# Score products of the recurrence as two half-width products per chunk instead of one full-width product

## The chip, the cores and the metric

The kernel runs on one core of one Trainium2 chip. The metric is the device time of one execution in microseconds (us), as the median of several runs. Each engine of the core has an instruction queue of its own that runs in order; in the profile PE is TensorE (matrix products), PEld its weight loads, DVE VectorE, ACT ScalarE, POOL GpSimd, SP SyncE, which issues most DMAs.

## The reference

Two layers of a diffusion backbone, in float32. Each layer mixes 768 tokens (256 context, 512 latent) through three parallel head groups (a gated recurrence in both directions, differential attention, a Fourier mix), and then runs a SwiGLU block. Only the recurrence matters here. Cut to its core, for one head (K = V = 128) and one direction:

```
def hgrn2_scan(q, v, z, lb, s0, reverse):
    f = lb + (1.0 - lb) * jax.nn.sigmoid(z)
    k, log_f = 1.0 - f, log(f)
    ...
def step(state, inp):                       # one chunk of tokens
    bcum = jnp.cumsum(gi, axis=2)
    o_inter = (qi * exp(bcum)) @ state
    decay = exp(where(incl, bcum[t] - bcum[s], -inf))
    scores = einsum('bhtk,bhsk,bhtsk->bhts', qi, ki, decay)
    o_intra = scores @ vi
    state = state * exp(blast) + (ki * exp(blast - bcum)).T @ vi
```

`scores[t, s]` has a decay that depends on both tokens and on the feature k, so it is no single matrix product.

## The kernel before

Every tensor lives in one SBUF arena that is cut into nine regions; `reg2f`, `reg6f` and so on in the profile are these regions (the digit is the region, f or r the kind of its contents), and `P` is PSUM, eight banks of 512 float32 columns. Large projections split each float32 operand into a high and a low float32r part and make three products per contraction block (`mm3`): these are the rows with `reg7r` (the weight stream's split pieces) and 256 or 512 columns. Weights come from HBM as 512 KB pieces in a fixed sequence, through three raw slots that ACT and DVE split (`pump`).

**The recurrence.** The kernel takes chunks of 128 tokens and builds both directions together. `gla_levels(h)` forms the 128x128 score block of each chunk by seven doubling levels: at level `lev`, with s = 2^lev, the pairs (t, s') whose indices differ first at bit `lev` take their score from a product of decayed keys and decayed queries; a mask per level says which entries of the block they are, and `copy_predicated` (line 787) lays them into the score block `osc`. Ahead of level 0 one more product per chunk gives the diagonal (`dst(1, c)`, put into `osc` by a plain ACT copy). So a head has one initial set of products, levels 0 to 5, and level 6: eight sets. A set makes one product for each chunk: six chunks in layer 0, four in layer 1. There are four heads and two layers.

The products of the initial set and of levels 0 to 5 are 128x128x128 in plain float32: the stationary operand is 128 keys of a chunk (`KM`, interleaved from the two directions by an ACT copy, `mixed`), the moving operand 128 queries read from `QP` by the view `dims`, runs of s words taken in turn from two places that lie s + T words apart (T = 768). The initial set reads `q` contiguously. At level 6 only the two quarters of the block off the diagonal have entries, and the kernel already makes them as two 64x64 products per chunk, with contiguous operands, into two partition halves of the bank. At all lower levels the entries that the mask takes lie in the two 64x64 quarters on the diagonal.

Between sets, DVE multiplies keys and queries by the gates, ACT interleaves the next `KM`, DVE lays the scores in. A plain float32 product is recorded as two MATMUL records (two passes), so a set of six full products shows as x12, and one of twelve half products as x24.

**Order of the work.** The program is recorded by generators. `drive` runs a main line (projections) and advances side lanes (`gla_levels`, `gla_post`, preparation of attention, attention, modulation) when a planner, the class `Clock`, says that their operands will be there. `mm` tells the planner what a product costs. `now` is the planner's time of PE. These numbers set only where independent instructions stand in each queue. `gla_post` runs after the levels of a head: transposes of keys, the states of the chunks, and `scores @ v` (rows with `reg5f`). `gemv` computes the modulation vectors of the next stage on PE from weight pieces of its own in the same stream (rows `32x512`).

Of the kernel before, what the change touches and what calls it, by code (L numbers as in the profile page):

```python
# [19 lines left out]
T = SEQ + CTX  # L20
# [9 lines left out]
# arena (float32 words per partition)  # L30
# [14 lines left out]
class Layout:  # L45
    """Constant area at the end of the arena."""
# [31 lines left out]
class Clock:  # L78
    """Expected times of the engines (ns); they only decide the order in which independent work is issued."""

    # from the end of a result to its use, by the engine that uses it
# [7 lines left out]
    def cells(self, ap):  # L89
        """tensor name and words of an access pattern"""  # L90
        dims = [(d[0], d[1]) for d in ap.ap]
        key = (ap.tensor.name, ap.offset, tuple(dims))
        if key not in self.known:
            ps = dims[0][0]
            starts, width = [ap.offset % ps if ps else ap.offset], 1
            for st, n in dims[1:]:
                if st >= 64 and n <= 16:
                    starts = [o + st * i for o in starts for i in range(n)]
                else:
                    width += st * (n - 1)  # L100
            idx = np.unique(np.concatenate([np.arange(o, o + width) for o in starts]))
            self.known[key] = (ap.tensor.name, idx)
        return self.known[key]
# [37 lines left out]
    def free(self, b):  # L141
        """when the tensor engine can write a bank that the other engines used"""
        return max([v for e, v in self.bank.get(b, {}).items() if e != 'pe'], default=0.0) + self.LAT['pe']

    def written(self, ap):
        """when the tensor engine can read it"""
        name, idx = self.cells(ap)
        return float(self.of(self.w, name)[idx].max()) + self.LAT['pe']


class Builder:
    def __init__(self, tc, ctx, ins, out):
        self.tc, self.nc, self.ins, self.out = tc, tc.nc, ins, out
        nc = self.nc
        gp = ctx.enter_context(tc.tile_pool(name="arena", bufs=1))
        pp = ctx.enter_context(tc.tile_pool(name="psum", bufs=1, space=bass.MemoryType.PSUM))
        self.L = Layout()
        self.gp = gp
        # (start, end, kind): r regions feed float32r products and are written rounded only
        cuts = [A0, A0 + 6144, B0, B0 + 6144, C0, VB, X0, W0, RAW0, self.L.end]  # L160
        self.reg = [[a, b, None, None] for a, b in zip(cuts, cuts[1:])]
        for i, k in enumerate('rrfffffrf'):
            self.mode(i, k)
        self.M = gp.tile([128, 7, 128], U8, name="M")
        self.P = pp.tile([128, 4096], F32, name="P")
        p0 = self.P[:, 0:1]
        self.pt, self.poff, self.pps = p0.tensor, p0.offset, p0.ap[0][0]
        self.sides = []
        self.ck = Clock()
        self.ready = {}  # L170
        self.have, self.gated = set(), set()

# [1 line left out]
    def mode(self, i, k):  # L174
        """Region i starts over with another kind of contents."""
        a, b, _, old = self.reg[i]
        if old != k:
            t = self.gp.tile([128, b - a], F32, tag=f"reg{i}", name=f"reg{i}{k}")
            self.reg[i] = [a, b, t, k]
# [42 lines left out]
    def mm(self, out, lhsT, rhs, start=True, stop=True):  # L222
        n, m = self.cols(rhs), self.cols(lhsT)
        if rhs.dtype == F32R:
            t = max(0.417 * n, 105)
        elif m == 32:
            t = 0.5 * n
        elif m == 64 and n == 64:
            t = 112
        else:  # L230
            t = 425 if n < 96 else max(215, 1.69 * n)
        self.ck.op('pe', t, [out], [lhsT, rhs])
        self.nc.tensor.matmul(out, lhsT, rhs, start=start, stop=stop)  # L233
# [61 lines left out]
    def rsqrt_mean(self, dst, src, n, w):  # L295
        """dst = (src / n + eps) ** -0.5 on w columns."""
        g, mh = self.nc.gpsimd, self.S(self.L.mh, w)
        self.ck.op('po', 160, [dst], [src])
        g.tensor_scalar(out=dst, in0=src, scalar1=1.0 / n, scalar2=EPS, op0=ALU.mult, op1=ALU.add)
        self.pool(dst, dst, mh, ALU.pow, 300 + 165 * w)  # L300

# [1 line left out]
    def step(self, lane):  # L303
        """Advance one lane of side work; it is due again when its results are expected."""
        self.ck.last = 0.0
        try:
            r = next(lane[0])
            self.ready[id(lane)] = r or self.ck.last
        except StopIteration:
            lane.pop(0)  # L310
# [18 lines left out]
    def drive(self, main, drain=True):  # L329
        for c in main:  # L330
            if isinstance(c, float):
                # side work goes first while a bank is still being read
                while c > self.now:
                    b = self.due(True)
                    if b is None or b[0] >= c:
                        break
                    self.step_any()
                continue
# [8 lines left out]
            n = 0  # L347
# [74 lines left out]
    def pump(self, upto=-1):  # L422
        seq, go = self.seq, True
        while go:
# [9 lines left out]
            if (self.n_proc < self.n_dma and seq[self.n_proc][2] < self.n_freed + NW  # L434
# [6 lines left out]
                if self.sides[2] and self.nbk == 2:  # L441
                    # VectorE is the busier one beside the attention
                    self.pool(self.r(self.S(w + 1024, 1024)), rw, self.S(w, 1024), ALU.subtract, 1920)
                else:
                    self.tt(self.r(self.S(w + 1024, 1024)), rw, self.S(w, 1024), ALU.subtract)
# [4 lines left out]
    def get(self):  # L450
        """Next split piece of the stream: offset of its high part (low part 1024 further)."""
# [28 lines left out]
    def extra_time(self):  # L480
        """when its next step can run, if that is known"""
# [12 lines left out]
    def more(self, n=1, force=False):  # L494
        """Take steps of the modulation that runs beside the main line."""
# [14 lines left out]
    def gemv(self, mods, src, free, b, wr):  # L510
        """silu(cond) @ w_mod[l][:, m] as feature columns; one step per piece and per result."""
# [33 lines left out]
    def gemv_v(self, mods, src, free, b, acc):  # L545
        """the same beside the main line: products and partial sums on VectorE, sums over the partitions at the end"""
# [44 lines left out]
    def gate(self, l, m, goff, after=None):  # L591
        """gate * norm_g broadcast over the partitions."""
# [16 lines left out]
    def norm(self, t, junk):  # L609
        """reciprocal root mean squares of a token tile"""  # L610
# [7 lines left out]
    def normed(self, t):  # L618
        """when they are there"""
        return self.ck.written(self.S(self.L.st + t, 1)) - 250  # L620

    def scaled(self, t, y):
        """normalized tile"""
# [4 lines left out]
    def turned(self, y):  # L628
        """when the tensor engine can turn it"""
        return max(self.ck.written(self.S(o, 512)) for o in y)  # L630

    def turn(self, y, b0, b1):
        """feature-major"""
# [33 lines left out]
    def spare(self):  # L667
        """bank that the modulation leaves to short work"""
        return 3 if self.nbk == 2 and self.extra is None and not self.sides[2] else self.aux()

    def aux(self):
        """bank for short work beside an accumulation of the main line"""
# [49 lines left out]
    def osc(self, h, c):  # L722
        """score block of chunk c"""
# [5 lines left out]
    def gla_levels(self, h):  # L729
# [26 lines left out]
        yield  # L756
        for c in chunks:
            self.mm(dst(1, c), self.S(self.osc(h, c), 128), self.S(q + c * 128, 128))
# [5 lines left out]
        for lev in range(7):  # L764
            s = 1 << lev
            nb = T // (2 * s)
            dims = ((2 * s, 64 // s), (s + T, 2), (1, s))
            for c in chunks:
# [5 lines left out]
                else:  # L774
                    self.mm(dst(lev, c), self.S(KM + 128 * c, 128), self.V(QP + 128 * c, *dims))
# [97 lines left out]
    def prep(self, b):  # L873
        """rope and exact split of k0, q0, k1, q1"""
# [26 lines left out]
    def stack(self, b):  # L901
        """per head and map: high and low parts in three blocks of 32 rows"""
# [8 lines left out]
    def attention(self):  # L911
# [18 lines left out]
        def scores(i):  # L930
# [3 lines left out]
            # the second map starts within a bank while the modulation holds bank 3  # L934
# [107 lines left out]
    def mixer(self):  # L1042
# [17 lines left out]
        for h in range(4):  # L1060
            if l and h == 2:
                # work that needs no buffer of the recurrence
# [45 lines left out]
        for b in range(4):  # L1108
            def kcb(bk, o, n):
                while self.n_prep < b:  # L1110
                    self.step(self.lane)
                # queries carry the negated scale of the scores
# [23 lines left out]
    def rest(self):  # L1136
        """end of the modulation that ran beside the projections"""
# [6 lines left out]
    def fnet(self, ut, us):  # L1144
# [3 lines left out]
        # tokens of one parity per tile: the two halves of the output are sum and difference of two transforms  # L1148
# [41 lines left out]
    def mix(self, t, c0, n, src, w, sc, b):  # L1190
        """feature-major split mix for one token tile"""
# [113 lines left out]
    def ffn(self):  # L1305
# [35 lines left out]
        for gi, g in enumerate(self.groups):  # L1341
            first = 0
            if gi == 0:
                # token quarters first, as they become ready
                wp = [(self.get(), self.get()) for _ in range(2)]
                parts = [(256, 256), (512, 256)] + ([(0, 256)] if l == 0 else [])
                for o, n in parts:
# [4 lines left out]
                    for i in range(2):  # L1352
                        if o == 256 and i:
                            # banks that the output projection has left
# [84 lines left out]
    def start(self):  # L1439
# [25 lines left out]
        nc.vector.memset(self.S(L.condT, 256), 0.0)  # L1465
        self.act(self.V(L.condT, (32, 8), (1, 2)), self.V(L.u, (2, 8), (1, 2)), AF.Silu)
# [48 lines left out]
    def columns(self):  # L1515
        """small per-feature constants"""
# [155 lines left out]
```

## Time and profile before

| | |
|---|---|
| runs | 1925.99 us median of 3 (1924.34 to 1930.29) |
| profiled execution | span 1923.9 us, from first to last instruction; 25,373 instructions |
| around the span | no time of that execution is given apart; the lowest run is 0.4 us above the span, the median 2.1 us |
| PE | 1833.2 us busy, 95% of the span |
| DVE, ACT, POOL | 54%, 35%, 9% |
| granted TensorE clock | 0.984 of full speed over the span |
| recurrence, layer 0 | from about 109 to 290 us |
| recurrence, layer 1 | from about 1200 to 1345 us |

The page divides the time by engine, by 40 slices and by the chain of work that ended last. The timeline gives start, length and count of merged instructions, so the distance from one start to the next is what a step costs PE; matmuls are pipelined, and their lengths overlap.

### The profile page before, as it was taken

The page shows a single profiled execution, that of the slowest core. Times are in us where ns is not written, and L with a number is a line of the kernel's source. Part 1 is how long each engine was busy: PE and PEld are TensorE (multiplying, and loading weights), DVE is VectorE, ACT ScalarE, POOL GpSimd, SP SyncE. Part 2 cuts the span into 40 slices and gives each one's busy share as a digit, 9 for nine tenths or more (in the row PEclk, how much of TensorE's full clock was granted, in tenths as well). Part 3 has the DMA queues.
Part 4 walks back from the last instruction along what each step waited for, and adds up shares of the span by engine and source line. Part 5 has one row for each costly group of instructions (what it writes and reads, how often), then busy time and mean ns, then how long its engine had stood idle before and what let it go on. Part 6 is the DMA issues. An engine that isn't in the chain of part 4 may idle for free.

```text
span 1923.9 us, 25373 instructions
## 1 busy us (share of the span) xinstructions
PE 1833.2 (95%) x10164; PEld 1544.5 (80%) x10164; DVE 1041.6 (54%) x1771; ACT 677.7 (35%) x1374; POOL 167.7 (9%) x244
## 2 busy tenths in 40 slices
PE   6999998996999999999999999999897989999998
PEld 3889995675789888888888878889676778888886
DVE  3477752565465666555455374876475553344344
ACT  4533331254564321212212273333255553232222
POOL 0000002112120000000000040000321210000002
PEclk8999999998999999999999999999998999999999
DMA  8211109435042443434343212111542123233321
GB/s 335 66 45 44 34 25 203 129 76 97 1 148 68 145 155 99 152 112 143 110 143 109 66 44 77 44 53 51 85 56 52 44 81 106 77 120 99 96 91 55
DMA packets 52390, 179.76 MB, mean 93 GB/s; under 512 B 6576, under 2 KB 7472, under 8 KB 52272
## 3 DMA queue, kind: packets, MB, share of 16 engines
q1 hardware_dynamic: 48816, 169.48, 27.2%
q0 software_dynamic: 3456, 8.65, 4.5%
q8 instruction: 80, 1.31, 0.3%
q14 instruction: 38, 0.31, 0.1%
HBM read 167.36 MB, written 2.10 MB: 88 GB/s over the span
## 4 chain that ended last, share of the span: by engine, by line
PE 85%; ACT 4%; DMA 4%; DVE 3%; issue 2%; POOL 1%; SPq 0%; DVEq 0%; POOLq 0%; ACTq 0%
PE P L233 82%; PE P L243 3%; ACT reg1f L254 1%; DMA reg8f<-in_wmod 1%; DMA reg2r<-reg5r 1%; ACT reg3f L254 1%; DMA reg8f<-in_wout 1%; ACT reg7r L254 1%; DVE reg7r L261 1%; DMA reg0r<-reg5r 1%; DMA reg4f<-in_wmod 0%; DVE reg8f L949 0%; POOL reg7r L281 0%; DVE reg4f L261 0%; DMA reg2f<-in_wmod 0%
## 5 line engine op out<-in xcount | busy, mean ns | idle before, releaser
L233 PE MATMUL P<-reg2r,reg7r 128*128 128x256 f32 (+1 forms) x1920 | 481.3, 338 | 0.0
L233 PE MATMUL P<-reg0r,reg7r 128*128 128x512 f32 (+1 forms) x1344 | 380.7, 363 | 3.9 <-ACT reg0r L254 3.9
L233 PEld LDWEIGHTS P<-reg2r,reg7r 128*128 128x128 f32 x1920 | 330.6, 190 | 37.8 <-issue 0.7
L261 DVE TENSOR_TENSOR reg7r<-reg8f,reg7r 128x1024 fp32r<-128x1024 f32 x191 | 233.0, 1230 | 228.7 <-ACT reg7r L254 227.4
L254 ACT ACTIVATE reg7r<-reg8f 128x1024 fp32r<-128x1024 f32 x204 | 212.7, 1054 | 378.4 <-issue 144.7
L233 PE MATMUL P<-reg7r,reg0r 128*128 128x512 f32 (+1 forms) x1272 | 328.7, 389 | 6.9 <-ACT reg0r L254 5.9
L233 PE MATMUL P<-reg3r,reg7r 128*128 128x512 f32 (+1 forms) x960 | 321.8, 335 | 0.4 <-DVE reg3r L261 0.4
L233 PEld LDWEIGHTS P<-reg0r,reg7r 128*128 128x128 f32 x1344 | 242.8, 191 | 51.3 <-issue 9.9
L233 PEld LDWEIGHTS P<-reg7r,reg0r 128*128 128x128 f32 x1272 | 232.8, 190 | 55.7 <-ACT reg0r L254 6.8
L233 PE MATMUL P<-reg1r,reg7r 128*128 128x512 f32 (+1 forms) x672 | 241.1, 359 | 0.6 <-DVE reg1r L261 0.6
L233 PE MATMUL P<-reg7r,reg2r 128*128 128x512 f32 (+1 forms) x912 | 232.7, 383 | 2.8 <-ACT reg2r L254 1.5
L233 PEld LDWEIGHTS P<-reg3r,reg7r 128*128 128x128 f32 x960 | 182.6, 190 | 18.6 <-issue 0.7
L233 PEld LDWEIGHTS P<-reg7r,reg2r 128*128 128x128 f32 x912 | 165.8, 189 | 36.0 <-ACT reg2r L254 3.1
L233 PEld LDWEIGHTS P<-reg1r,reg7r 128*128 128x128 f32 x672 | 128.2, 191 | 18.9 <-DVE reg1r L261 1.1
L273 DVE SCALAR_TENSOR_TENSOR reg8f<-reg8f 128x512 f32<-128x512 f32 (+3 forms) x154 | 88.9, 577 | 11.3 <-DMA reg8f<-in_wmod 8.3
L949 DVE TENSOR_REDUCE reg8f<-P 128x1 f32<-128x768 f32 (+1 forms) x80 | 64.2, 843 | 52.8 <-PE P L233 52.8
L233 PE MATMUL P<-reg7r,reg1r 128*128 128x512 f32 (+1 forms) x240 | 90.7, 378 | 0.1
L254 ACT ACTIVATE reg3f<-P,reg8f 128x768 f32<-128x768 f32 (+3 forms) x96 | 51.2, 570 | 84.9 <-DVE reg8f L949 40.7
L281 POOL TENSOR_TENSOR reg8f<-reg8f 128x1 f32<-128x1 f32 (+2 forms) x102 | 60.9, 599 | 162.6 <-ACT reg5f L254 78.5
L233 PE MATMUL P<-reg7r,reg3r 128*128 128x512 f32 (+1 forms) x192 | 70.4, 367 | 1.5 <-DVE reg3r L273 1.5
L254 ACT ACTIVATE reg0r<-reg1f 128x256 fp32r<-128x256 f32 (+1 forms) x46 | 23.5, 511 | 132.1 <-DVE reg1f L261 132.1
L261 DVE TENSOR_TENSOR reg5f<-reg5f,P 128x512 f32<-128x512 f32 x60 | 40.9, 686 | 47.3 <-PE P L233 47.2
(213 smaller groups left out, 2064.5 us busy)
## 6 DMA issues: line engine op xcount, KB each, us to landing
reg8f<-in_wfi SPq DMA_DIRECT2D x88, 512.0 KB, 3.6
reg8f<-in_wmod SPq DMA_DIRECT2D x80, 512.0 KB, 3.7
reg8f<-in_win SPq DMA_DIRECT2D x56, 512.0 KB, 3.6
reg8f<-in_wfo SPq DMA_DIRECT2D x44, 512.0 KB, 3.6
reg8f<-in_wout SPq DMA_DIRECT2D x16, 512.0 KB, 3.9
reg6f<-in_xin SPq DMA_DIRECT2D x12, 512.0 KB, 6.4
reg2r<-reg5r POOLq DMA_DIRECT2D x12, 384.0 KB, 9.6
reg2f<-in_wmod SPq DMA_DIRECT2D x8, 512.0 KB, 6.4
```

What stands on the lines that cost most here:

```text
L233: self.nc.tensor.matmul(out, lhsT, rhs, start=start, stop=stop)
L243: self.nc.tensor.transpose(out, in_, self.S(self.L.ident, 128))
L254: self.nc.scalar.activation(out=out, in_=in_, func=func, **kw)
L261: self.nc.vector.tensor_tensor(out=out, in0=a, in1=b, op=op)
L273: self.nc.vector.scalar_tensor_tensor(out=out, in0=a, scalar=s, in1=b, op0=op0, op1=op1)
L281: self.nc.gpsimd.tensor_tensor(out=out, in0=a, in1=b, op=op)
L949: self.nc.vector.tensor_reduce(out=sm(i, 2 + m), in_=x, axis=AX.X, op=ALU.min)
```

## The change

The initial set and levels 0 to 5 make two products per chunk, one for each 64x64 quarter on the diagonal: 64 keys stationary, 64 queries moving, into partitions 0 to 63 and 64 to 127 of the same bank. The view `dims` has half the number of runs. The quarters off the diagonal are no longer written at these levels; since the copy of the initial set and `copy_predicated` still read whole 128x128 blocks, `start` zeroes three PSUM banks once. The planner's cost of a 64x64 product is 56 ns in place of 112, and 150 ns are added whenever a product with fewer than 128 stationary columns follows one with 128, or the reverse (`gemv` with 32 columns counts too). Comment lines are dropped as well; they are left out here.

```diff
@@ Builder.__init__
         self.ready = {}
+        self.narrow = False
@@ mm
         elif m == 64 and n == 64:
-            t = 112
+            t = 56
         else:
             t = 425 if n < 96 else max(215, 1.69 * n)
-        self.ck.op('pe', t, [out], [lhsT, rhs])
+
+        self.ck.op('pe', t + 150 * ((m < 128) != self.narrow), [out], [lhsT, rhs])
+        self.narrow = m < 128
@@ gla_levels
         for c in chunks:
-            self.mm(dst(1, c), self.S(self.osc(h, c), 128), self.S(q + c * 128, 128))
+            for hf in (0, 64):
+                self.mm(dst(1, c, hf, 64)[hf:hf + 64], self.S(self.osc(h, c) + hf, 64), self.S(q + c * 128 + hf, 64))
@@ gla_levels
-            dims = ((2 * s, 64 // s), (s + T, 2), (1, s))
+            dims = ((2 * s, 32 // s), (s + T, 2), (1, s))
@@ gla_levels
                 else:
-                    self.mm(dst(lev, c), self.S(KM + 128 * c, 128), self.V(QP + 128 * c, *dims))
+                    for hf in (0, 64):
+                        self.mm(dst(lev, c, hf, 64)[hf:hf + 64], self.S(KM + 128 * c + hf, 64), self.V(QP + 128 * c + hf, *dims))
@@ start
         nc.vector.memset(self.S(L.condT, 256), 0.0)
+
+        nc.vector.memset(self.W(3 * 512, 3 * 512), 0.0)
```

The planner's numbers also move instructions. On PE in the first head of layer 0, around its level 4 set (`reg2f,reg6f`; the other rows are a projection), before:

```order
302 L233 MATMUL P<-reg1r,reg7r 128x512
303 L233 MATMUL P<-reg0r,reg7r 128x512
304 L233 MATMUL P<-reg2f,reg6f 128x128 x6
305 L233 MATMUL P<-reg0r,reg7r 128x512
306 L233 MATMUL P<-reg1r,reg7r 128x512
```

and after the change:

```order
302 L236 MATMUL P<-reg1r,reg7r 128x512
303 L236 MATMUL P<-reg0r,reg7r 128x512 x2
304 L236 MATMUL P<-reg1r,reg7r 128x512
305 L236 MATMUL P<-reg0r,reg7r 128x512 x2
306 L236 MATMUL P<-reg1r,reg7r 128x512
307 L236 MATMUL P<-reg0r,reg7r 128x512
308 L236 MATMUL P<-reg2f,reg6f 64x64 x12
```

The set stands six projection products later in the queue, and it is twelve half products instead of six whole ones. Sets all along the recurrence move in this way by some products, earlier or later.

On PE in layer 0 beside the attention (`reg2r` is attention scores, `reg6f,reg3f` and `reg8f,reg3f` are attention too, `reg7r,reg0r` and `reg7r,reg1r` a projection), around the last `gemv` products of the modulation (`reg8f 32x512`), before:

```order
1066 L233 MATMUL P<-reg6f,reg3f 128x128 x6
1067 L243 MATMUL P<-reg8f,reg3f 128x128 x6
1068 L233 MATMUL P<-reg7r,reg0r 128x512 x2
1069 L233 MATMUL P<-reg7r,reg1r 128x512
1070 L233 MATMUL P<-reg7r,reg0r 128x512 x2
1071 L233 MATMUL P<-reg7r,reg1r 128x512
1072 L233 MATMUL P<-reg8f 32x512 x2
1073 L233 MATMUL P<-reg7r,reg0r 128x512 x2
```

and after:

```order
1081 L236 MATMUL P<-reg6f,reg3f 128x128 x6
1082 L246 MATMUL P<-reg8f,reg3f 128x128 x6
1083 L236 MATMUL P<-reg7r,reg0r 128x512 x2
1084 L236 MATMUL P<-reg7r,reg1r 128x512
1085 L236 MATMUL P<-reg7r,reg0r 128x512 x2
1086 L236 MATMUL P<-reg7r,reg1r 128x512
1087 L236 MATMUL P<-reg8f 32x512 x2
1088 L236 MATMUL P<-reg7r,reg0r 128x512 x2
1089 L236 MATMUL P<-reg7r,reg1r 128x512
1090 L236 MATMUL P<-reg7r,reg0r 128x512 x2
1091 L236 MATMUL P<-reg7r,reg1r 128x512
1092 L236 MATMUL P<-reg8f 32x512 x2
```

The last `gemv` products stand at row 1092 instead of 1072; between the two places lie 18 projection products, four score products, six plain products and six transposes. The transposes that end the modulation stand at row 1102 instead of 1086. From row 1105 of before (1107 of after) on the two orders agree again until layer 1's recurrence, and the orders on SP and POOL are the same throughout.

## Rows read from the trace of the kernel before

**Rows 1.** The cores: span, mean granted clock.
```profile
core 0: 1923.9 us, clock 0.984
```

**Rows 2.** The page: engines' busy time, the chain, one costly DVE group.
```profile
PE 1833.2 (95%) x10164; PEld 1544.5 (80%) x10164; DVE 1041.6 (54%) x1771; ACT 677.7 (35%) x1374; POOL 167.7 (9%) x244
...
PE 85%; ACT 4%; DMA 4%; DVE 3%; issue 2%; POOL 1%; SPq 0%; DVEq 0%; POOLq 0%; ACTq 0%
...
L261 DVE TENSOR_TENSOR reg5f<-reg5f,P 128x512 f32<-128x512 f32 x60 | 40.9, 686 | 47.3 <-PE P L233 47.2
```

**Rows 3.** Windows: length, busy us of PE, PEld, DVE, ACT, POOL, PEclk, DMA.
```profile
0.00:18.00 18.00, 10.83 (x42) 2.30 (x44) 0.63 (x3) 3.40 (x7) 0.31 (x5) 1.00 0.89 343
109.00:146.00 37.00, 37.00 (x265) 33.49 (x264) 30.19 (x61) 13.14 (x22) 0.00 (x0) 1.00 0.14 42
300.00:345.00 45.00, 37.08 (x168) 22.92 (x167) 15.98 (x26) 6.19 (x10) 12.92 (x13) 0.92 0.93 191
1232.00:1265.00 33.00, 33.00 (x235) 30.02 (x234) 27.28 (x61) 11.72 (x28) 1.55 (x2) 1.00 0.15 49
```

**Rows 4.** Timeline of PE, layer 0, level 5: start, length, instruction.
```profile
134.05 0.28 PE L233 MATMUL P<-reg0r,reg7r 128*128 128x256 f32 x1
134.17 1.50 PE L233 MATMUL P<-reg2f,reg6f 128*128 128x128 f32 x12
135.43 0.36 PE L233 MATMUL P<-reg0r,reg7r 128*128 128x256 f32 x1
135.63 0.28 PE L233 MATMUL P<-reg1r,reg7r 128*128 128x256 f32 x1
```

**Rows 5.** Timeline of PE, layer 0, level 6 of the second head.
```profile
172.54 0.28 PE L233 MATMUL P<-reg0r,reg7r 128*128 128x256 f32 x1
172.75 0.92 PE L233 MATMUL P<-reg2f,reg3f 128*64 128x64 f32 x24
173.60 0.39 PE L233 MATMUL P<-reg0r,reg7r 128*128 128x256 f32 x1
173.82 0.28 PE L233 MATMUL P<-reg1r,reg7r 128*128 128x256 f32 x1
```

**Rows 6.** Timeline of PE, layer 0: levels 0 and 1 of the first head.
```profile
113.17 2.16 PE L233 MATMUL P<-reg2f,reg6f 128*128 128x128 f32 x12
115.03 0.54 PE L233 MATMUL P<-reg0r,reg7r 128*128 128x512 f32 x1
...
119.27 1.61 PE L233 MATMUL P<-reg2f,reg6f 128*128 128x128 f32 x12
120.62 0.38 PE L233 MATMUL P<-reg0r,reg7r 128*128 128x256 f32 x1
```

**Rows 7.** Timeline of PE, layer 1: level 0, level 1, and a coarser level.
```profile
1203.93 1.49 PE L233 MATMUL P<-reg0f,reg8f 128*128 128x128 f32 x8
1205.12 0.53 PE L233 MATMUL P<-reg2r,reg7r 128*128 128x512 f32 x1
...
1208.03 1.13 PE L233 MATMUL P<-reg0f,reg8f 128*128 128x128 f32 x8
1208.90 0.49 PE L233 MATMUL P<-reg2r,reg7r 128*128 128x512 f32 x1
...
1245.58 1.05 PE L233 MATMUL P<-reg0f,reg8f 128*128 128x128 f32 x8
1246.39 0.36 PE L233 MATMUL P<-reg2r,reg7r 128*128 128x256 f32 x1
```

**Rows 8.** Timeline of PE, layer 1: level 6 of the last head.
```profile
1330.32 0.69 PE L233 MATMUL P<-reg0f,reg1f 128*64 128x64 f32 x16
1330.93 0.50 PE L233 MATMUL P<-reg7r,reg2r 128*128 128x256 f32 x2
```

**Rows 9.** Chain in order of time, layer 0 beside the attention.
```profile
322.78 11.36 DMA reg8f<-in_wmod
...
428.80 18.07 DMA reg2r<-reg5r
```

## The prediction

> **What bounds the kernel now.** I read the cores first: one core, 1923.9 us at a mean granted clock of 0.984 [rows 1]. Then the page: PE is busy for 95% of the span and makes up 85% of the chain that ended last [rows 2], so what is taken off PE's queue counts unless something else is late just there. Then the windows of the stages that the change touches. A stretch of 37.0 us with the first head of layer 0 has PE busy for all of it, DVE for 30.2 us; one of 33.0 us in layer 1 has PE busy for all of it and DVE for 27.3 us. The DMA share is 0.14 and 0.15 and the clock 1.00 [rows 3]. So the recurrence is bound by PE: the sets of score products are slipped between projection products that fill whatever the chain through DVE and ACT leaves open. Last the timeline of PE around single sets, where the distances from start to start are the prices.
>
> **The price of a full set.** At level 5 in layer 0 the last projection product ahead starts at 134.05, the set at 134.17, the next projection product at 135.43, the one after it at 135.63 [rows 4]. Of the 1.58 us from the first to the last start, two projection products of 0.12 us (134.05 to 134.17) belong to the main line, so a full set of twelve passes costs 1.34 us; its body, from its start to the next one's, is 1.26 us. In layer 1 eight passes have a body of 0.81 us (1245.58 to 1246.39) [rows 7]. The difference is 0.45 us for four passes, so 112 ns per pass.
>
> **The price of a half-width set.** Level 6 has the shape that the change gives to all others: 24 passes of 64 columns from 172.75 to 173.60, a body of 0.85 us; from 172.54 to 173.82 are 1.28 us, less 0.24 is a cost of 1.04 us [rows 5]. Sixteen passes in layer 1 have a body of 0.61 us (1330.32 to 1330.93) [rows 8]. The difference of 0.24 us for eight passes gives 30 ns per pass, and a body is 0.13 us plus 30 ns per pass. Outside the body a half-width set costs 0.19 us (1.04 less 0.85), a full one 0.08 (1.34 less 1.26), so going in and out costs 0.11 us more.
>
> Gain of a set that runs like level 6: in layer 0 1.34 - 1.04 = 0.30 us, in layer 1 (0.81 - 0.61) - 0.11 = 0.09 us. A set breaks even at (1.26 - 0.11 - 0.13) / 24 = 42 ns per pass in layer 0 and at 36 ns in layer 1.
>
> A rule of the Trainium skill speaks against such a gain: the page "TensorE: Matmul & The Clock Gate", section "The mechanism", says that a weight load overlaps a running product only when the two use different row groups, and here both halves use all 128 rows. By that rule a pass would cost its load and its stream in turn, and the sets would get dearer. Level 6 shows 30 ns per pass with the same rows in use, so the measurement decides against it for contiguous operands.
>
> **What differs from level 6: the moving view.** In the levels 0 to 5 the queries come in runs of 2^lev words from two places in turn; at level 6 and in the initial set they are contiguous. The full sets show what the runs cost. Levels 2 to 5 have the price of a contiguous read (level 5, rows 4). Level 0 has a body of 1.86 us for twelve passes (113.17 to 115.03) and level 1 of 1.35 us (119.27 to 120.62) [rows 6]; in layer 1 they have 1.19 and 0.87 us for eight [rows 7]. That is (1.86 - 1.19) / 4 = 168 ns and (1.35 - 0.87) / 4 = 120 ns per pass: at level 0 the read sets the pace, at level 1 barely. No row shows a half-width pass with such a view, so I bound it. A pass of 64 columns needs half the time of a full one, 84, 60 and 56 ns at level 0, level 1 and the others. If consecutive passes, which go to different partition halves, run two at a time, the price per pass is half of that, 42, 30 and (as at level 6) 30 ns. If such reads come one after another, it is the whole. I take two at a time: half of a full contiguous pass is 56 ns, and level 6 runs at 30, so there the passes do overlap in pairs, and a slower read by each of the two does not by itself end that.
>
> The Trainium skill has a reason for level 0 to be slow: the page "SBUF — State Buffer", section "Door 1: The DMA port swizzle (why `[64,N]` ≈ `[32,N]`)", says that SBUF is read in lines of 16 bytes and that fewer than two accesses to a line cost bandwidth. Runs of one word do that at level 0 alone, and the rows agree (168 ns against 112). Whether two overlapping reads share that penalty no row here shows.
>
> **The sum.** Layer 0, per head: five sets that run like level 6 (the initial one, levels 2 to 5) give 5 x 0.30 = 1.50 us. Level 1 gives 1.35 - 0.85 - 0.11 = 0.39. Level 0 has a new body of 0.13 + 24 x 0.042 = 1.14 and gives 1.86 - 1.14 - 0.11 = 0.61. Together 2.50, for four heads 10.0 us. Layer 1, per head: 5 x 0.09 = 0.45; level 1 0.87 - 0.61 - 0.11 = 0.15; level 0 with 0.13 + 16 x 0.042 = 0.80 gives 1.19 - 0.80 - 0.11 = 0.28. Together 0.88, for four heads 3.5 us. In all 13.5 us.
>
> **The other parts.** The bank memset at the start is one DVE instruction of 1536 columns, some 3 x 0.69 = 2.1 us by the nearest row with a PSUM operand [rows 2]. DVE is busy for 0.63 us of the first 18 [rows 3] and the zeroed banks are first written later, so it costs nothing; without that cover, 2.1 us. `copy_predicated` and the ACT copies keep their sizes. DVE keeps its work while its head gets shorter: 37.0 - 2.5 = 34.5 us against 30.2 of DVE work, and 33.0 - 0.9 = 32.1 against 27.3. So PE still ends last; if DVE did, the first head could lose at most what its stretch has left, and the other heads of layer 0 have longer ones. The planner's new costs move sets by a few projection products, which have no wait of their own.
>
> Where the saved time arrives: after layer 0's recurrence comes a stage in which the chain runs through weight DMAs, with a DMA share of 0.93 from 300 to 345 us [rows 3] and single waits of 11.4 us for a modulation weight and 18.1 us for the attention's stacked operands [rows 9]. These transfers start when PE or attention frees a slot or ends a step; in the recurrence ahead the queue is nearly idle (0.14). So this stage should start 10 us earlier and keep its length. What speaks against it is the modulation, whose end is queued 16 to 20 rows later beside the same attention work; its weight slots come free later, and behind them wait the Fourier and output weights in SP's queue. Between row 1072 and row 1092 lie 18 projection and four score products at twice the 0.12 us of 256 columns, six plain products at 1.26 us and six transposes at no more than half of that: 4.3 + 1.0 + 1.3 + 0.6 = 7.2 us by which the modulation can end later, all of it or none hidden by the slack ahead of the output projection. I take nothing lost.
>
> The profiled span of 1923.9 becomes 1910.4; the median of the runs lies 2.1 us above the span, so **1912.5 us**.
>
> **The rivals.**
> - *The two finest levels do not overlap.* Bodies by whole passes: level 0 0.13 + 24 x 0.084 = 2.15 and level 1 1.57 us in layer 0, 1.47 and 1.09 in layer 1. They lose 0.40, 0.33, 0.39 and 0.33 us. Per head layer 0 then gives 1.50 - 0.73 = 0.77 and layer 1 0.45 - 0.72 = -0.27; in all 2.0 us, 1924.0. For it: these are the levels whose full passes are already slower. Chance 0.16.
> - *No strided pass overlaps* (slower). Levels 2 to 5 at 56 ns have bodies of 1.48 and 1.03 us and lose 0.33 each in both layers. Per head 0.30 - 0.73 - 1.32 = -1.75 and 0.09 - 0.72 - 1.32 = -1.95, in all 14.8 us more: 1940.8. It decides from 42 ns per pass on. Against it: at levels 2 to 5 the full passes cost no more than contiguous ones. The rule on row groups above would end on this side too. Chance 0.09.
> - *The modulation's late end takes back part of layer 0's gain*, at most the 7.2 us above: 1912.5 + 7.2 = 1919.7. For it: DMA ends several waits in that stage; against it: the orders meet again some 15 rows later. Chance 0.13.
> - *Nothing arrives*: DVE's chain or a DMA fills what PE leaves: 1926. Against it: PE is busy in all of both stretches. Chance 0.05.
>
> **How the numbers follow.** My forecast has the remaining chance of 0.57, with a range of its own from 1908 to 1917 (the waits of the DMA stage may move by some 4 us either way). From 1907 to 1925 the first, the second and the fourth case (modulation) are taken in, 0.86 with their edges cut to about 0.8; the slower case stays out. About 0.3% (6 us) is what a measurement of this kernel can tell from no change. Faster by more: my case and half of the modulation's, 0.64. Within: the finest levels, the other half, nothing arrives, about 0.24. Slower: 0.12, with a small part for stalls from the new order.
>
> **What would show it.** In the profile after: sets of x24 and x16 with a body of 0.85 and 0.61 us at levels 2 to 5 and in the initial set; about 1.14 and 0.80 us at level 0; PE still busy throughout both recurrences; the attention of layer 0 some 10 us earlier. A body near 2.1 us at level 0, one above 1.1 us at levels 2 to 5, or longer DMA waits between 300 and 450 us would each prove the step of that name wrong.

## The result and the profile after

| | before | after |
|---|---|---|
| median of the runs | 1928.14 us (4 runs, 1924.34 to 1934.03) | 1914.8 us (4 runs, 1910.43 to 1916.13) |
| profiled span | 1923.9 us | 1908.6 us |

The ratio is 0.9931, with a 95% interval from 0.9906 to 0.9955: faster by 13.3 us. 1912.5 was forecast, from a median of 1925.99 us before, which a fourth run moved to 1928.14. The interval means a gain of 8.7 to 18.1 us; that 13.3 lies so near the 13.5 that were forecast is closer than these runs can tell.

The span became 15.3 us shorter (the profiled run of after is its fastest, 1910.43 us). To see where, I cut it at four places that both profiles have: the first set of layer 0, the PE piece that the chain shows behind layer 0's recurrence (60 products), the first set of layer 1, and the PE piece behind layer 1's recurrence (144 products). The chain in order of time, start and length, before:

```profile
300.20 13.06 PE P L233 x60
...
1342.47 26.35 PE P L233 x144
```

and after:

```profile
286.97 13.06 PE P L236 x60
300.04 10.76 DMA reg8f<-in_wmod
...
414.86 17.53 DMA reg2r<-reg5r
...
1326.95 26.33 PE P L236 x144
```

The sets themselves, from the timeline of PE after (start, length, instruction, in brackets the idle time ahead and what ended it). First layer 0 with levels 0, 1 and 2, and level 6 of the first head; then layer 1 with the initial set, levels 0 and 1, and last the end of its recurrence:

```profile
111.25 1.22 PE L236 MATMUL P<-reg2f,reg6f 128*64 128x64 f32 x24
112.40 0.50 PE L236 MATMUL P<-reg0r,reg7r 128*128 128x512 f32 x1
...
116.71 0.96 PE L236 MATMUL P<-reg2f,reg6f 128*64 128x64 f32 x24
117.61 0.39 PE L236 MATMUL P<-reg0r,reg7r 128*128 128x256 f32 x1
...
119.75 0.28 PE L236 MATMUL P<-reg0r,reg7r 128*128 128x256 f32 x1
119.96 0.92 PE L236 MATMUL P<-reg2f,reg6f 128*64 128x64 f32 x24
120.81 0.39 PE L236 MATMUL P<-reg0r,reg7r 128*128 128x256 f32 x1
121.03 0.28 PE L236 MATMUL P<-reg1r,reg7r 128*128 128x256 f32 x1
...
134.41 0.92 PE L236 MATMUL P<-reg2f,reg3f 128*64 128x64 f32 x24 [0.87 <-DVE reg6f L793]
...
1186.91 0.69 PE L236 MATMUL P<-reg1f,reg8f 128*64 128x64 f32 x16
1187.53 0.39 PE L236 MATMUL P<-reg2r,reg7r 128*128 128x256 f32 x1
...
1190.55 0.88 PE L236 MATMUL P<-reg0f,reg8f 128*64 128x64 f32 x16
1191.35 0.50 PE L236 MATMUL P<-reg2r,reg7r 128*128 128x512 f32 x1
...
1195.66 0.71 PE L236 MATMUL P<-reg0f,reg8f 128*64 128x64 f32 x16
1196.30 0.39 PE L236 MATMUL P<-reg2r,reg7r 128*128 128x256 f32 x1
...
1322.32 2.05 PE L236 MATMUL P<-reg5f,reg1f 128*128 128x128 f32 x16 [1.37 <-ACT reg1f L257]
1326.05 0.72 PE L236 MATMUL P<-reg5f,reg1f 128*128 128x128 f32 x4 [1.68 <-DVE reg1f L276]
1326.95 0.49 PE L236 MATMUL P<-reg5f,reg6f 128*128 128x128 f32 x2 [0.18 <-DVE reg1f L276]
```

Start to start gives the bodies. A contiguous set or one at level 2 has 0.85 us (119.96 to 120.81) where a full one had 1.26 [rows 4]; in layer 1 it is 0.62 us (1186.91 to 1187.53) against 0.81 [rows 7]. Going in and out costs what it cost at level 6: 119.75 to 121.03 is 1.28 us, less two projection products of 0.12 and the body of 0.85 leaves 0.19 [rows 5]. Level 0 has 1.15 and 0.80 us, level 1 has 0.90 and 0.64, against 1.86, 1.19, 1.35 and 0.87 of before [rows 6, 7].

The windows of after (length, busy us of PE, PEld, DVE, ACT, POOL, PEclk, DMA share, GB/s), the first head of layer 0 and the second of layer 1:

```profile
108.00:143.00 35.00, 34.02 (x346) 28.28 (x346) 30.80 (x62) 13.07 (x22) 0.00 (x0) 1.00 0.16 47
...
1219.00:1251.00 32.00, 32.00 (x291) 27.32 (x290) 25.74 (x59) 11.84 (x29) 1.23 (x2) 1.00 0.16 49
```

PE is still what bounds both recurrences, but the first head of layer 0 now shows the next limit: DVE is busy for 30.8 of 35.0 us, and PE waits once, 0.87 us, for `copy_predicated` ahead of level 6.

### The profile page after: what moved, and what is told of

It reads as the page before. It is cut to its first block, busy times and chain, and to the rows that moved or that the text cites. A ratio compares the mean times of both kernels' runs of the same rounds, so it can differ in the third digit from the quotient of the medians.

```text
span 1908.6 us, 26494 instructions
## 1 busy us (share of the span) xinstructions
PE 1819.4 (95%) x10724; PEld 1516.4 (79%) x10724; DVE 1040.9 (55%) x1772; ACT 677.3 (35%) x1374; POOL 168.1 (9%) x244
## 4 chain that ended last, share of the span: by engine, by line
PE 85%; ACT 4%; DMA 4%; DVE 4%; issue 1%; POOL 1%; SPq 0%; DVEq 0%; POOLq 0%; ACTq 0%
PE P L236 82%; PE P L246 3%; ACT reg1f L257 1%; DMA reg8f<-in_wmod 1%; ACT reg3f L257 1%; DMA reg2r<-reg5r 1%; DMA reg8f<-in_wout 1%; ACT reg7r L257 1%; DMA reg0r<-reg5r 1%; DVE reg7r L264 1%; DMA reg4f<-in_wmod 0%; DVE reg8f L955 0%; POOL reg7r L284 0%; DVE reg4f L264 0%; DMA reg2f<-in_wmod 0%
```

## Where the time came from

The same cuts in the profiles of three experiments, all in us (the experiments follow below):

| kernel | up to the first set | layer 0's recurrence | between | layer 1's recurrence | from there to the end |
|---|---|---|---|---|---|
| before | 109.73 | 190.47 | 900.01 | 142.26 | 581.4 |
| after | 108.11 | 178.86 | 899.94 | 140.04 | 581.7 |
| `halves_old_order` | 109.73 | 180.30 | 901.03 | 138.45 | 585.0 |
| `full_new_order` | 108.36 | 189.50 | 898.53 | 143.70 | 582.9 |
| `quarters` | 108.86 | 174.11 | 899.85 | 134.10 | 586.6 |

Of the 15.3 us, 11.6 come from layer 0's recurrence and 2.2 from layer 1's. The 1.6 us ahead of the first set are not the change's: PE's order up to there is the same. Right behind a wait of 1.9 us for ACT, the same row of projection products runs in both kernels, from 44.19 to 55.59 us before and from 43.84 to 53.86 after: 11.40 and 10.02 us. The windows of that place (columns as above), before:

```profile
44.00:56.00 12.00, 11.81 (x46) 9.30 (x47) 5.54 (x11) 8.61 (x20) 1.86 (x6) 0.86 0.24 90
```

and after:

```profile
44.00:56.00 12.00, 11.93 (x60) 9.81 (x61) 6.56 (x14) 9.22 (x23) 1.87 (x6) 1.00 0.29 101
```

The granted clock is 0.86 before, so part of the stretch ran at 1.2 GHz, and 1.00 after, all of it at 2.4 GHz. `halves_grouped`, which has half products too, shows 0.86 there again. The last column varies by 5 us among kernels that run the same PE instructions in the same order in it; that is taken up at the end.

## The experiments

The theories to tell apart: the time comes from half products that run two at a time (mine); it comes from the new order; or it comes from something in the sets that would not need alternation. Each kernel was timed beside the kernel before on the same chip.

**Half products in the old order.** The planner's costs are chosen so that every instruction stands where it stood before.

```diff
         elif m == 64 and n == 64:
-            t = 56
+            t = self.t64          # 108, at level 6 112
-        self.ck.op('pe', t + 150 * ((m < 128) != self.narrow), [out], [lhsT, rhs])
+        self.ck.op('pe', t, [out], [lhsT, rhs])
```

> The half-width products and the memset as in the change, but with planner costs that leave every instruction where it stood before (108 ns per half product, no switch cost). If the gain is the price of the sets alone, the span is the one after the change within about 2 us: some 13 us below before, near 0.993 of it. If the new order brought part of it, the gain is smaller: the sets alone were worked out at 10.0 us in layer 0 and 3.5 in layer 1, and what layer 0 gained beyond 10 us must then be missing.

1914.98 us (6 runs, 1911.82 to 1916.32) against 1927.65 (17 runs): ratio 0.9933, interval 0.9917 to 0.995. The sets alone carry the whole change: layer 0 becomes 10.2 us shorter (190.47 to 180.30) and layer 1 3.8 us (142.26 to 138.45), where 10.0 and 3.5 were forecast.

**Full products in the new order.** The products of before, and the planner's costs of after.

```diff
-    def mm(self, out, lhsT, rhs, start=True, stop=True):
+    def mm(self, out, lhsT, rhs, start=True, stop=True, score=False):
...
+        if score:
+            t, m = 112, 64
```

> The full-width products of before, but in the order that the changed planner gives. If the gain is the price of the sets, this runs as before within 2 us (ratio 1.000). If the order matters by itself, the time falls by some us (order helps) or rises by up to 7 us (the modulation that ends later beside the attention delays the stage from 300 to 450 us).

1927.99 us (12 runs, 1924.31 to 1929.56): ratio 1.0001, interval 0.9989 to 1.0012. The order is worth nothing as a whole, but not in each place. Layer 0 is 1.0 us shorter (with half products 1.4: 180.30 to 178.86), layer 1 is 1.4 us longer (with half products 1.6). The loss has a place, the end of layer 1's recurrence. PE's waits there are 1.36, 1.68 and 0.18 us in `full_new_order`, and in after the three that the timeline above shows (1322.32 to 1326.95). In the old order they are two, as the timeline of `halves_old_order` has it:

```profile
1327.81 0.72 PE L237 MATMUL P<-reg5f,reg1f 128*128 128x128 f32 x4 [0.96 <-DVE reg1f L277]
1329.51 0.49 PE L237 MATMUL P<-reg5f,reg6f 128*128 128x128 f32 x2 [0.98 <-DVE reg1f L277]
```

In the new order, with full or half products, PE waits 3.2 us for the states of the last head, in the old order 1.9: the projection products that used to stand between have been issued earlier, and 1.3 us of the 1.4 to 1.6 are this. In layer 0 PE's waits inside the recurrence are 0.9 us in after and 1.9 in `halves_old_order`, so 1.0 of the 1.4 us gained there are waits; the rest I have not traced.

**Half products, grouped.** All products of one half of a set, then all of the other.

```diff
-        for c in chunks:
-            for hf in (0, 64):
+        for hf in (0, 64):
+            for c in chunks:
```

> As after the change, but a set makes the products of one partition half for all chunks and then those of the other, so that consecutive products use the same half. If half-width passes are cheap because passes to different halves run in pairs, a pass costs about 56 ns at most levels and 84 at level 0: bodies of about 1.48 and 2.15 us in layer 0, 1.03 and 1.47 in layer 1, and the time is some 25 us above the changed kernel. If a pass of 64 columns is cheap by itself, the bodies stay at 0.85, 1.15, 0.61 and 0.80 us and the time too.

1939.3 us (one run), 24.5 us above after. Timeline of PE: the initial set and level 0 in layer 0, then in layer 1:

```profile
109.89 1.43 PE L236 MATMUL P<-reg3f,reg6f 128*64 128x64 f32 x24
111.26 0.38 PE L236 MATMUL P<-reg0r,reg7r 128*128 128x256 f32 x1
...
113.55 1.92 PE L236 MATMUL P<-reg2f,reg6f 128*64 128x64 f32 x24
115.40 0.50 PE L236 MATMUL P<-reg0r,reg7r 128*128 128x512 f32 x1
...
1203.77 0.97 PE L236 MATMUL P<-reg1f,reg8f 128*64 128x64 f32 x16
1204.67 0.38 PE L236 MATMUL P<-reg2r,reg7r 128*128 128x256 f32 x1
...
1207.68 1.24 PE L236 MATMUL P<-reg0f,reg8f 128*64 128x64 f32 x16
1208.85 0.50 PE L236 MATMUL P<-reg2r,reg7r 128*128 128x512 f32 x1
```

Level 0 has 1.85 and 1.17 us, so (1.85 - 1.17) / 8 = 85 ns per pass; a contiguous set has 1.37 us in layer 0 and 0.90 us in layer 1, 59 ns per pass (58 by the starts of the single records in the trace, which the timeline merges). Per pass these are the whole prices, 84 and 56 ns, by which the prediction bounded a pass that overlaps with none. The same products in turn between the halves cost (1.15 - 0.80) / 8 = 44 and 30 ns in after. So the gain comes from the alternation of partition halves, at level 0 as elsewhere, and with the grouped loop the change would have been slower than before.

The bodies came out below the 2.15, 1.48, 1.47 and 1.03 us that were expected, and the single records show why. In layer 0's level 0 set the starts fall, by their rhythm, into two streams of twelve, with 84 ns between the starts of each. The second stream, the other half, begins at 114.260, while the first runs on to 114.510: the starts there are 114.254, 114.260, 114.339, 114.379, 114.425, 114.464. So at the join of the two halves their passes run side by side, ahead of the order of the program and although they belong to different chunks. What counts is the partition half, and not that the neighbour in the alternating loop belongs to the same chunk. In after's level 2 set two passes start 7 ns apart, and the next two 58 ns behind them.

**Other queries, contiguous.** To price the strided read of levels 0 and 1.

```diff
-  self.mm(dst(lev, c, hf, 64)[hf:hf + 64], self.S(KM + 128 * c + hf, 64), self.V(QP + 128 * c + hf, *dims))
+  self.mm(dst(lev, c, hf, 64)[hf:hf + 64], self.S(KM + 128 * c + hf, 64), self.S(QP + 128 * c + hf, 64))
```

> As after the change, but the queries of levels 0 to 5 are read as 64 contiguous words, so that the scores take other queries than they should; everything else is the same. If the runs of one word are what makes level 0 dearer, its body falls from 1.15 to 0.85 us (0.80 to 0.61 in layer 1) and level 1's from 0.90 to 0.85; if it is its place after the initial set, it stays.

1914.45 us (one run). Level 0 in layer 0, timeline of PE:

```profile
111.08 0.92 PE L236 MATMUL P<-reg2f,reg6f 128*64 128x64 f32 x24
111.92 0.50 PE L236 MATMUL P<-reg0r,reg7r 128*128 128x512 f32 x1
```

A body of 0.84 us instead of 1.15 (in layer 1 0.62 instead of 0.80): the runs of one word, and nothing else of level 0, make it dearer. The two recurrences became 1.0 and 0.9 us shorter, of (4 x 0.31) + (4 x 0.06) + (4 x 0.18) + (4 x 0.02) = 2.3 us that the bodies of levels 0 and 1 give. The time of the whole run does not resolve that.

**Quarters.** The diagonal quarters are themselves made of 32x32 blocks: up to level 4 four products of 32 keys and 32 queries hold all entries. The planner is told 28 ns each.

```diff
-            for hf in (0, 64):
-                self.mm(dst(1, c, hf, 64)[hf:hf + 64], self.S(self.osc(h, c) + hf, 64), self.S(q + c * 128 + hf, 64))
+            for hf in range(0, 128, 32):
+                self.mm(dst(1, c, hf, 32)[hf:hf + 32], self.S(self.osc(h, c) + hf, 32), self.S(q + c * 128 + hf, 32))
...
+            w = 32 if lev < 5 else 64
```

> As after the change, but the initial set and levels 0 to 4 make four 32x32 products per chunk in place of two of 64x64. If a pass costs its columns plus some 3 ns, 48 passes of about 17 ns give a body near 0.9 us, as with halves, and level 0 gets somewhat cheaper: time within 4 us of the changed kernel. If there is a floor near 30 ns per pass whatever its columns, the body is 0.13 + 48 x 0.030 = 1.57 us in layer 0 and 1.09 in layer 1, and the time is some 25 us above the changed kernel.

1906.52 us (4 runs, 1905.25 to 1908.65): ratio 0.9895, interval 0.9872 to 0.9918. The initial set and level 0 in layer 0, then in layer 1 (timeline of PE):

```profile
108.86 0.63 PE L236 MATMUL P<-reg3f,reg6f 128*32 128x32 f32 x48
109.42 0.39 PE L236 MATMUL P<-reg0r,reg7r 128*128 128x256 f32 x1
...
111.72 0.72 PE L236 MATMUL P<-reg2f,reg6f 128*32 128x32 f32 x48
112.36 0.50 PE L236 MATMUL P<-reg0r,reg7r 128*128 128x512 f32 x1
...
1182.82 0.46 PE L236 MATMUL P<-reg1f,reg8f 128*32 128x32 f32 x32
1183.20 0.39 PE L236 MATMUL P<-reg2r,reg7r 128*128 128x256 f32 x1
...
1186.22 0.54 PE L236 MATMUL P<-reg0f,reg8f 128*32 128x32 f32 x32
1186.69 0.50 PE L236 MATMUL P<-reg2r,reg7r 128*128 128x512 f32 x1
```

The bodies are 0.56 and 0.38 us; their difference gives (0.56 - 0.38) / 16 = 11 ns per pass, and level 0 has the same slope, (0.64 - 0.47) / 16. Neither of the expected prices came out: the passes are cheaper than both. How they run shows in layer 1's initial set if its timeline is cut at 1182.890, 1182.922 and 1182.954:

```profile
1182.82 0.27 PE L236 MATMUL P<-reg1f,reg8f 128*32 128x32 f32 x8
1182.82 0.30 PE L236 MATMUL P<-reg1f,reg8f 128*32 128x32 f32 x12
1182.82 0.33 PE L236 MATMUL P<-reg1f,reg8f 128*32 128x32 f32 x16
```

Four passes start every 32 ns, so a contiguous pass costs 8 ns in turn and not 11. By the single records layer 0's contiguous sets keep this rhythm for their first 32 passes; behind them some 50 ns are lost, which the difference of the bodies counts as price. Why they are lost is open. At level 0 four passes start every 44 ns, in both layers and to the end of the set: 11 ns per pass.

By the bodies layer 0 should gain 4 x (4 x 0.29 + 0.34 + 0.51) = 8.0 us on after; 4.8 arrived (178.86 to 174.11). PE's waits inside that recurrence are 3.6 us instead of 0.9 (3.4 of it in nine waits for `copy_predicated`), which is 2.7 of the 3.2 us missing. In layer 1, where DVE has fewer chunks, all arrives: 4 x (4 x 0.22 + 0.25 + 0.33) = 5.8 us by the bodies, 5.9 measured.

**Quarters, grouped.** All products of one quarter, then the next.

```diff
-        for c in chunks:
-            for hf in (0, 64):
+        for hf in range(0, 128, 32):
+            for c in chunks:
```

> As with quarters, but all chunks of one partition group first, then the next group. Gives the price of a 32-column pass alone. If a pass alone costs its columns plus a few ns as at 64 columns (58 ns) and 128 (112 ns), it is about 31 ns: bodies of 0.13 + 48 x 0.031 = 1.6 us in layer 0 and 1.1 in layer 1, against 0.56 and 0.39, and three passes ran at a time with quarters. If it is 11 ns alone, the bodies stay and the groups play no part.

1936.06 us (one run). Timeline of PE, the initial set in layer 0 and in layer 1:

```profile
108.88 1.41 PE L236 MATMUL P<-reg3f,reg6f 128*32 128x32 f32 x48
110.21 0.39 PE L236 MATMUL P<-reg0r,reg7r 128*128 128x256 f32 x1
...
1203.66 0.90 PE L236 MATMUL P<-reg1f,reg8f 128*32 128x32 f32 x32
1204.49 0.39 PE L236 MATMUL P<-reg2r,reg7r 128*128 128x256 f32 x1
```

One after another a pass of 32 columns costs (1.33 - 0.83) / 16 = 31 ns; at level 0 the bodies are 1.70 and 1.00 us, 44 ns per pass. In turn four start in 32 ns, at level 0 four in 44 ns: all four quarters run at a time, and not the three that the expectation took from 11 ns.

**Quarters at level 5, and at level 6.** Level 5 as four contiguous 32x32 products taken straight from the keys and queries, which also drops its ACT copy; then level 6 as four products of 32 keys and 64 queries.

```diff
+                elif lev == 5:
+                    for k in range(4):
+                        hf, j = k % 2, k ^ 1
+                        o = dst(lev, c, 32 * j, 32)
+                        self.mm(o[32 * k:32 * k + 32], self.S(KS + T * hf + 128 * c + 32 * k, 32),
+                                self.S(QP + T * (1 - hf) + 128 * c + 32 * j, 32))
...
-            if lev < 5:
+            if lev < 4:
```

> As with quarters, and level 5 too: four 32x32 products per chunk, keys and queries read contiguously as at level 6, which drops eight ACT copies as well. By the bodies that quarters showed (0.56 us for 48 passes, 0.39 for 32) level 5 falls from 0.85 and 0.61 us to these: (0.29 + 0.22) x 4 = 2.0 us less on PE. If PE still bounds the recurrence, some 2 us below quarters; if DVE's chain does by now (PE already waits for copy_predicated there), the same as quarters.

> As quarters_lev5, and level 6 as four products of 32 keys by 64 queries per chunk. If as many passes run at a time as there are different partition groups in a row, 48 passes of 64 columns take 58 / 4 = 14.5 ns each, body 0.83 us as against 0.85 now: no difference. If only two streams fit at a time, 30 ns each, body 1.57 us: 4 us slower over both layers.

With level 5: 1904.68 us (4 runs, 1901.17 to 1907.57), ratio 0.9877, interval 0.9861 to 0.9894, the lowest median of all and below both kernels. With level 6 as well: 1905.08 us, ratio 0.9881 (0.9866 to 0.9895), no difference. Level 6 in the latter has a body of 0.81 us instead of 0.85, as expected for four passes of 64 columns at a time (0.83) and not for two (1.57). It stands behind a wait for DVE of 1.27 us in the first head. The step from `quarters` to level 5 is within the intervals, and in layer 0 of the kernel with level 5 PE waits 3.8 us for `copy_predicated`: with quarters DVE has become the engine that the first head waits for. Its window in the kernel with level 5 (columns as above):

```profile
105.00:140.00 35.00, 32.60 (x513) 26.99 (x512) 30.64 (x62) 12.46 (x20) 0.00 (x0) 1.00 0.16 55
```

## Why the prediction was right, point by point

- **The bound.** PE was busy through both recurrences, and what was taken off its queue arrived. The forecast sum of 13.5 us stands against 14.0 with the order held (10.2 and 3.8), 13.8 in the two recurrences of after, and 13.3 in the medians.
- **A half-width set like level 6: 0.85 and 0.61 us, 0.11 us dearer in and out.** Confirmed to 0.01 us for the contiguous sets (0.85 and 0.62).
- **Level 0 at 42 ns per pass.** 44 ns: 1.15 and 0.80 us where 1.14 and 0.80 were forecast.
- **Level 1 at 0.85 and 0.61 us.** A little too low: 0.90 and 0.64, 32 ns per pass. With the 0.01 at level 0, the terms of levels 0 and 1 were together 0.09 us per pair of heads too large, 0.4 us in all. The measured 14.0 is still above the sum: by the new bodies and the forecast's 0.11 it would be 13.2. The order is the same in before and `halves_old_order`, so their single records can be compared one by one: the 56 sets, each with the product ahead and the one behind, give 10.4 and 3.6 us, the whole 14.0. Of the 0.8 us some 0.5 are level 0's. Going in and out costs it mostly 0.06 us and not 0.11 (0.71 us less body, 0.65 us gained), and the full set of layer 0's second head took 2.08 us. The rest are mostly waits between the sets.
- **Two at a time.** This was the assumption on which the two first rivals turned, and the grouped kernel settles it: 58 and 85 ns alone, 30 and 44 ns in turn. The rival of slow finest levels and that in which no strided pass overlaps have the prices per pass of the grouped loop, not of this one.
- **The rule on row groups.** All products here use all 128 rows, and the time of a pass is halved or not by whether its neighbour goes to the other partition half. The Trainium skill, page "TensorE: Matmul & The Clock Gate", section "The mechanism", says that a weight load overlaps a running product only when the two use different row groups. By that rule after would be no faster than the grouped kernel (1.37 us per contiguous set); the rows show 0.85, and the measurement decides.
- **Runs of one word.** That level 0 is dearer because of them was argued and is now shown (0.84 us with contiguous queries). This agrees with the Trainium skill, page "SBUF — State Buffer", section "Door 1: The DMA port swizzle (why `[64,N]` ≈ `[32,N]`)", by which fewer than two accesses to a line of 16 bytes cost bandwidth: runs of one word cost 44 ns per pass in turn, runs of two words 32, contiguous ones 30. The open point was whether two overlapping reads share the penalty. They don't: 85 ns alone is 44 ns in pairs, as cleanly halved as 58 is to 30.
- **The moved instructions at no cost.** Right in sum, ratio 1.0001, and wrong in its reason: moved sets do make waits, 1.3 us of them at the end of layer 1, and save about as much in layer 0. That 1.4 us more in layer 0 and 1.6 us less in layer 1 leave the forecast sum as it was is luck.
- **The modulation's late end.** Up to 7.2 us were at stake. The stretch between the recurrences is 900.01 us before and 899.94 after, and 898.53 with full products in the new order: nothing is lost. The delay itself came: the transposes that end the modulation start 101.5 us behind the cut after layer 0's recurrence before (at 401.67) and 109.3 us behind it after (at 396.28), 7.8 us later. But the stacked operands, for which PE waits longest there, land 146.7 and 145.4 us behind the same cut, and that slack hides all of it. Of the waits that were named, the one for the stacked operands became 0.5 us shorter in the chain (18.07 to 17.53) [rows 9]. Modulation weights make two: 8.28 and 11.36 us before, 10.76 and 9.98 after, 1.1 us longer in sum, while PE itself idles 7.9 us for them before and 7.4 after.
- **DVE's chain.** The cover that the prediction counted, 34.5 us of head against 30.2 us of DVE work, held but for one wait of 0.87 us.

## What to carry to other kernels

Here small plain float32 products whose results go to different partition groups ran beside each other when the loop sent neighbours to different groups. Write that loop innermost: grouped by partition a pass cost twice (halves, 58 ns against 30) or four times (quarters, 31 against 8) as much. Cut a masked product to the blocks that the mask takes, as finely as the price of going in and out (0.11 us per set here) and the next engine allow: here DVE's `copy_predicated` took back a third of what the quarters freed in layer 0. And before an unmeasured shape is called a risk, look for the same shape elsewhere in the trace: level 6 gave the price of five other sets to 0.01 us.

## What the runs showed of the hardware that was not expected

- A pass of 32 columns costs 31 ns alone and 8 ns when four partition quarters take turns; with the strided read of level 0 it is 44 and 11 ns. Four run at a time in both cases, and the dearer read is shared like the rest.
- The granted clock behind a wait differs between kernels whose PE instructions are the same there. Behind layer 1's recurrence PE waits 3.9 us for the stacked operands (4.0 in `quarters`). Windows of 5 us from there on (columns as above, PEclk the third value from the end), in after:

```profile
1363.60:1368.60 5.00, 4.37 (x14) 3.60 (x15) 3.56 (x5) 1.88 (x4) 0.00 (x0) 0.66 0.11 40
1368.60:1373.60 5.00, 5.00 (x24) 4.12 (x23) 0.00 (x0) 1.55 (x2) 2.39 (x1) 1.00 0.00 0
```

and in `quarters`:

```profile
1355.40:1360.40 5.00, 4.99 (x13) 4.03 (x14) 2.81 (x4) 1.87 (x4) 0.00 (x0) 0.50 0.09 33
1360.40:1365.40 5.00, 5.00 (x21) 4.02 (x20) 0.00 (x0) 1.54 (x2) 1.59 (x1) 0.85 0.00 0
```

  In `quarters` PE ran the first 5 us wholly at 1.2 GHz and was granted 0.67 once more 15 us later, among three waits of 1.9 us in all for ACT and DVE; in after the clock was back at 2.4 GHz in the second window and stayed. `halves_old_order` looks like `quarters` (0.52, 0.80, later 0.73), before looks like after. Over 40 us from the end of that wait the granted clock is 0.88 in `quarters` and `halves_old_order`, 0.96 in after and before. That is 8% of 40 us, an estimate of 3.2 us of the 3 to 5 us by which the last stage differs in the table. In `quarters` the 144 products ahead of the wait also took 1.6 us longer (27.97 us at a granted clock of 0.94, in after 26.33 at 1.00). Runs of one kernel differ too: of 17 runs of before the shortest span, 1919.8 us, has a mean clock of 0.986 and the longest, 1930.3 us, one of 0.980. Why it falls one way in one kernel's profile and the other way in another's stays open: each kernel has one profile.
